# Sharing out half projections between attention steps: three each in the first pair of heads

## Chip, core and metric

The kernel runs on one core of one Trainium2 chip. Its time is device microseconds (us) of one execution; lower is better. The profile comes from one further execution with the hardware profiler on.

## What is computed

One layer of a decoder trunk with 512 tokens of width 1024, in float32. The part that matters here is the first half of it:

```python
h = rms_norm(x, norm_mix[l])
proj = h @ w_in[l]
q_a, k_a, v_a, u_b, gate_b, gate_c, g_a, g_b = jnp.split(proj, split_points, axis=-1)
...
o_a = stick_breaking_attention(heads(q_a), heads(k_a), heads(v_a))   # 8 heads x 64, causal
y_b = gate_b * causal_depthwise_conv(gate_c * u_b, conv_w[l])
branch_a = o_a @ w_branch_a[l]
branch_b = y_b @ w_branch_b[l]
merged = jax.nn.sigmoid(g_a) * branch_a + jax.nn.sigmoid(g_b) * branch_b
x = x + merged @ w_mix_out[l]
```

The attention is

```python
z = jnp.einsum('bhqd,bhkd->bhqk', qb, kb) * scale
mask = k_pos < q_pos
log_fail = jnp.where(mask, jax.nn.log_sigmoid(-z), 0.0)
log_later = lax.cumsum(log_fail, axis=3, reverse=True) - log_fail
weights = jnp.where(mask, jnp.exp(jax.nn.log_sigmoid(z) + log_later), 0.0)
out = jnp.einsum('bhqk,bhkd->bhqd', weights, vb)
```

A softmax cross-attention into 256 memory tokens, a SwiGLU layer and a final RMSNorm follow; the change doesn't touch them.

## The kernel before

**Arithmetic.** Every float32 operand of a matrix product is split into a high and a low part (`..h` and `..l` in tile names; ScalarE casts the high part, VectorE subtracts it for the low part), and each product is three matmuls: high with high, high with low, low with high (`mm3`, lines 154 to 157). Everything is held with channels on the 128 partitions and the 512 tokens along the free axis.

**Projections and halves.** A projection is 128 columns of `w_in`: 8 blocks of 128 input channels, three matmuls each, 24 matmuls into one PSUM tile `pr`. It is cut into two halves of 12 matmuls. `open_project` (line 270) loads the weights (DMA on SP into `wr`, cast to `wh` on ScalarE, `wl` on VectorE) and does the first half; `project` (line 276) does the second, and its caller evicts the PSUM tile on VectorE:

- `qk_part` (line 291): q or k of a pair of heads, scaled and split into `qkh`, `qkl`; for q, the half that belongs to the later 256 tokens is also copied into `lq` by four DMAs on SP (line 300).
- `conv` (line 311), three projections a pair: gate C (`gc`, line 315), the input u (`cu`, lines 321 and 322, then the three taps `cv`, lines 324 to 328), gate B (`gb`, lines 334 and 335, split into `yh`, `yl`).
- `gate` (line 304): merge gate A or B (called A0, B0, A1, B1 below for the first two blocks of 128 channels), evicted into `g` at line 307.

**Attention.** The 8 heads are 4 pairs, and each pair goes through 4 key tiles of 128 keys, from the last to the first: 16 steps (`steps`, line 341). Key tile `kt` has 512 - 128 `kt` queries to serve, so the four steps of a pair grow from 128 to 512 queries. A step has

- `scores` (line 373): TensorE writes z (lines 382 and 389); ScalarE and VectorE make e = log(1 + exp z) from it (lines 396 to 399), GpSimd masks it (`causal`, line 355).
- `parts` (line 408): VectorE adds to e what the key tiles behind it summed up (`carry`, line 420; it comes by a DMA, line 444, issued on SP from a row that `weights` of the step before left), and `lsplit` splits it into `l`: high on ScalarE (line 369), low on VectorE (line 370).
- `weights` (line 428): TensorE adds the cumulative sum of l to z by a triangular matrix (line 433); VectorE takes the next carry from it (line 438), ScalarE exponentiates into `a` (line 441), GpSimd masks, VectorE splits (`ah`, `al`, lines 449 and 450).
- `values` (line 454): TensorE multiplies with v (line 461); after a pair's last step the result `ot` is put together and split (lines 469 to 472).

**Order.** TensorE's order in the attention is the order of the program (`manual_schedule`, line 518). The loop over i, from 0 to 16, does in each iteration: the share of half projections (`fill_some`), `scores` of step i + 1, `weights` of step i, `parts` of step i + 1, `values` of step i - 1. ScalarE, VectorE, GpSimd and SP are ordered by the scheduler of the language when the kernel is built: the chain of a step (`scores`, `parts`, `weights`) has a raised priority, the evictions and splits of the projections have not.

The list `fill` holds 22 projections, so 44 halves, in the order q, k of the next pair, gate C, u, gate B of this pair, pair by pair, and then A0, B0, A1, B1. How many of them are done up to the end of iteration i's share is in two lines:

```python
shares = FILL[0] + (TT - 1) * FILL[1]
...
            fill_some(n_fill * sum(shares[:i + 1]) / sum(shares))
```

`n_fill` is 44; `FILL[0]` is the first pair's four shares, `FILL[1]` that of the other three pairs. `fill_some` goes on while fewer halves are done than its argument, so a fraction is rounded up.

**Buffers.** `pmm` has two PSUM banks. They hold the projections' `pr`, and in iteration 14 (`MEAN_AT`) also two small results on the memory tokens: `rm` (line 526; matmuls at line 188, read on ScalarE at lines 121 and 126), done between the share and the scores, and `rmb` (line 538; matmuls at line 197 into `varb`, read on ScalarE as `ry`, line 121, and on VectorE as `rv`, line 124), done at the iteration's end. `tpool` has seven buffers of 128x512, shared by e, a, qk, gc, cv, gb, g, ot and by the ry, rv and ra of `rmb`. A buffer is given out again when its last reader is done. g of a merge gate stays until its sigmoid, behind the attention.

After iteration 15 there is one more gate projection (line 532), the last values, and then the branches.

Of the kernel before, what the change touches and what calls it, by code (L numbers as in the profile page):

```python
# [29 lines left out]
MEM_AT = (5, 7, 9, 11)  # L30
MEAN_AT = 14
EARLY = 2
FILL = ((3, 2, 3, 3), (2, 2, 3, 4))
WARM = 8
FIRST = 4

# [4 lines left out]
def hybrid_layer(ctx: ExitStack, tc: tile.TileContext, xT_d, memT_d, cols_d, wv_d, win_d,  # L41
# [464 lines left out]
    n_fill = len(fill)  # L506
    shares = FILL[0] + (TT - 1) * FILL[1]

# [585 lines left out]
```

## Time and profile before

| what | value |
|---|---|
| median of three runs | 860.76 us (860.56 to 861.03) |
| the profiled execution | 860.98 us |
| its span, first to last instruction | 859.2 us |
| TensorE matmuls busy | 850.5 us, 99% of the span |
| VectorE busy | 586.5 us, 68% |
| ScalarE busy | 431.1 us, 50% |
| granted TensorE clock, mean | 0.999 |

Times in views of the profile count from the start of the span. The profile records the start of every matmul; the ends are modelled, and consecutive matmuls overlap in it. In a timeline a row has start, length, engine, line, operation, the tile written and those read, the shape, and the count of equal instructions merged into it; in brackets stands how long the engine idled before it and which instruction released it. "PEld" is TensorE's weight load.

### The profile page before, as it was taken

What the parts mean: (1) busy time and instruction counts of PE and PEld (TensorE: products, weight loads), DVE (VectorE), ACT (ScalarE), POOL (GpSimd) and SP (SyncE); (2) the same over time, 40 slices, a digit from 0 to 9 for tenths busy, and PEclk for the clock granted to TensorE, in tenths of its full rate; (3) what the DMA queues carried; (4) which work ended last, traced back from release to release, by engine and by line L of the source; (5) the groups of instructions that cost most, each with busy time, mean ns of one, the idle gap of its engine ahead of it and who ended that gap; (6) DMA issues with size and microseconds to landing.
All of it is one profiled execution on the core that took longest, in us unless ns stands there. A gap on an engine that the chain in (4) does not pass through costs nothing.

```text
span 859.2 us, 12693 instructions
## 1 busy us (share of the span) xinstructions
PE 850.5 (99%) x4912; PEld 748.6 (87%) x4912; DVE 586.5 (68%) x963; ACT 431.1 (50%) x750; POOL 62.0 (7%) x92
## 2 busy tenths in 40 slices
PE   9999999999999999999999999999999999999997
PEld 7877788888888898888888889999999999888897
DVE  8769898986454475555555779888887778533334
ACT  7566766665333344433444666555445556422335
POOL 1011111111000000000000101111111100000002
PEclk9999999999999999999999999999999999999999
DMA  8322331228333255422110527776777753322202
GB/s 295 132 90 77 120 111 62 74 99 266 111 103 111 96 177 184 143 98 98 50 67 33 137 54 202 187 182 172 185 188 195 182 147 127 119 98 99 73 1 98
DMA packets 42859, 108.34 MB, mean 126 GB/s; under 512 B 4656, under 2 KB 8752, under 8 KB 42800
## 3 DMA queue, kind: packets, MB, share of 16 engines
q1 hardware_dynamic: 36528, 95.72, 32.8%
q0 software_dynamic: 5984, 11.54, 8.2%
q8 instruction: 38, 0.62, 0.3%
q10 hardware_dynamic: 288, 0.29, 0.1%
q14 instruction: 21, 0.17, 0.1%
HBM read 104.36 MB, written 2.10 MB: 124 GB/s over the span
## 4 chain that ended last, share of the span: by engine, by line
PE 96%; DVE 2%; DMA 1%; issue 0%; POOL 0%; SPq 0%; DVEq 0%; ACT 0%; POOLq 0%
PE z L801 15%; PE y L801 7%; PE pr L155 7%; PE pr L156 7%; PE pr L157 7%; PE f L156 5%; PE f L157 5%; PE f L155 5%; PE v L801 4%; PE r L156 3%; PE r L155 3%; PE r L157 3%; PE v L261 3%; PE mq L156 2%; PE mq L157 2%; PE mq L155 2%
## 5 line engine op out<-in xcount | busy, mean ns | idle before, releaser
L150 ACT CAST wh<-wr 128x1024 fp32r<-128x1024 f32 x106 | 111.1, 1050 | 222.2 <-issue 98.6
L151 DVE TENSOR_TENSOR wl<-wr,wh 128x1024 fp32r<-128x1024 f32 x106 | 129.4, 1223 | 99.4 <-ACT wh L150 99.2
L155 PE MATMUL pr<-xgh,wh 128*128 128x512 f32 x288 | 112.6, 391 | 0.0
L156 PE MATMUL pr<-xgl,wh 128*128 128x512 f32 x288 | 112.4, 390 | 0.0
L157 PE MATMUL pr<-xgh,wl 128*128 128x512 f32 x288 | 112.3, 390 | 0.0
L156 PE MATMUL f<-actl,wh 128*128 128x512 f32 (+1 forms) x208 | 74.3, 357 | 0.0
L155 PE MATMUL f<-acth,wh 128*128 128x512 f32 (+1 forms) x208 | 74.2, 357 | 0.0
L157 PE MATMUL f<-acth,wl 128*128 128x512 f32 (+1 forms) x208 | 74.1, 357 | 0.0
L801 PE MATMUL z<-xdh,wf 128*128 128x256 f32 x352 | 70.4, 283 | 0.0
L157 PEld LDWEIGHTS pr<-xgh,wl 128*128 128x128 f32 x288 | 54.1, 188 | 11.3
L155 PEld LDWEIGHTS pr<-xgh,wh 128*128 128x128 f32 x288 | 54.1, 188 | 10.9
L156 PEld LDWEIGHTS pr<-xgl,wh 128*128 128x128 f32 x288 | 54.1, 188 | 10.8
L758 POOL DMA_DIRECT2D ws<-in_w_ffn_in_dram x22 | 26.6, 1208 | 469.0 <-DVE c L616 267.8
L801 PEld LDWEIGHTS z<-xdh,wf 128*128 128x128 f32 x352 | 58.0, 192 | 0.0
L821 ACT COPY sa<-z 128x256 f32<-128x256 f32 x44 | 16.4, 372 | 78.3 <-PE z L801 78.2
L801 PE MATMUL z<-xdl,wf 128*128 128x256 f32 x176 | 49.9, 283 | 0.0
L792 DVE TENSOR_TENSOR wf<-s,wf 128x512 fp32r<-128x512 f32 x44 | 30.3, 691 | 21.1 <-ACT wf L791 20.0
L155 PEld LDWEIGHTS f<-acth,wh 128*128 128x128 f32 x208 | 39.3, 189 | 5.8
L156 PEld LDWEIGHTS f<-actl,wh 128*128 128x128 f32 x208 | 39.3, 189 | 5.6
L157 PEld LDWEIGHTS f<-acth,wl 128*128 128x128 f32 x208 | 39.3, 189 | 5.5
L801 PE MATMUL v<-xoh,wf 128*128 128x256 f32 x176 | 35.5, 283 | 0.0
L801 PE MATMUL y<-xch,wf 128*128 128x256 f32 x176 | 35.5, 283 | 0.0
(281 smaller groups left out, 2134.8 us busy)
## 6 DMA issues: line engine op xcount, KB each, us to landing
wr<-in_w_in_dram SPq DMA_DIRECT2D x36, 512.0 KB, 3.3
ws<-in_w_ffn_in_dram SPq DMA_DIRECT2D x22, 512.0 KB, 3.8
wg<-in_w_ffn_in_dram SPq DMA_DIRECT2D x22, 512.0 KB, 4.2
ws<-in_w_ffn_in_dram POOLq DMA_DIRECT2D x22, 512.0 KB, 5.8
wr<-in_w_ffn_out_dram SPq DMA_DIRECT2D x22, 512.0 KB, 3.3
a<-in_w_ffn_in_dram SPq DMA_DIRECT2D x22, 256.0 KB, 4.5
wr<-in_w_branch_dram SPq DMA_DIRECT2D x8, 512.0 KB, 3.2
wr<-in_w_mem_k_dram SPq DMA_DIRECT2D x8, 512.0 KB, 3.2
```

The costliest lines, as they stand in the source:

```text
L150: after(nc.scalar.copy(h2, raw), lead[-1:])
L151: lows.append(nc.vector.tensor_tensor(out=l2, in0=raw, in1=f(h2), op=ALU.subtract))
L155: nc.tensor.matmul(ps, a[0], b[0], start=start, stop=False, **kw)
L156: nc.tensor.matmul(ps, a[0], b[1], start=False, stop=False, **kw)
L157: nc.tensor.matmul(ps, a[1], b[0], start=False, stop=stop, **kw)
L261: nc.tensor.matmul(vps[t], xg[k][a][:, sl], wv[k][b], start=k == 0 and (a, b) == (0, 0), stop=k == KD - 1 and a == 1)
L758: nc.gpsimd.dma_start(s13, a[:, 0:4:3, :], accum_op=ALU.add)
L792: nc.vector.tensor_tensor(out=lo, in0=raw, in1=f(hi), op=ALU.subtract)
L801: nc.tensor.matmul(ps[:, :HS], a, b, start=i < 3 and k == 0 and j == 0, stop=k == KP - 1 and j == 2, skip_group_check=True)
L821: nc.scalar.copy((s[:, :HS], None, None, s[:, HS:], t[:, :HS])[i], z)
```

## The change

```diff
-FILL = ((3, 2, 3, 3), (2, 2, 3, 4))
+FILL = ((3, 3, 3, 3), (2, 2, 3, 4))
```

The shares before add up to 44, the number of halves, so each iteration does just its number. After the change they add up to 45 for the same 44 halves, and with the rounding up the totals behind iterations 0 to 15 are:

```text
before  3 5 8 11   13 15 18 22   24 26 29 33   35 37 40 44
after   3 6 9 12   14 16 19 23   25 27 30 34   36 38 41 44
```

Iteration 1 does three halves instead of two, iteration 15 three instead of four, and all others as many as before. From iteration 1 on every half stands one place earlier. With "o" for the first half of a projection and "f" for the second one, GC, U and GB for the conv's three and q, k numbered by their pair from 0:

```text
i    before                after
0    oq1 fq1 ok1           oq1 fq1 ok1
1    fk1 oGC               fk1 oGC fGC
2    fGC oU fU             oU fU oGB
3    oGB fGB oq2           fGB oq2 fq2
4    fq2 ok2               ok2 fk2
5    fk2 oGC               oGC fGC
6    fGC oU fU             oU fU oGB
7    oGB fGB oq3 fq3       fGB oq3 fq3 ok3
8    ok3 fk3               fk3 oGC
9    oGC fGC               fGC oU
10   oU fU oGB             fU oGB fGB
11   fGB oGC fGC oU        oGC fGC oU fU
12   fU oGB                oGB fGB
13   fGB oA0               oA0 fA0
14   fA0 oB0 fB0           oB0 fB0 oA1
15   oA1 fA1 oB1 fB1       fA1 oB1 fB1
```

No matmul, load or other instruction is added or removed.

## Prediction, made before the changed kernel was run

> **What bounds the kernel now.** I read the page first, for the span, the engines and the chain; then the table by stretch, to see whether the stretch of the change is bound like the rest; then the waits of TensorE there; then the timeline of the attention steps one by one. i is the step loop's counter (line 519); step n is the pair and key tile whose scores are issued in iteration n-1 and whose weights in iteration n.
>
> ```profile
> span 859.2 us, 12693 instructions
> PE 850.5 (99%) x4912; PEld 748.6 (87%) x4912; DVE 586.5 (68%) x963; ACT 431.1 (50%) x750; POOL 62.0 (7%) x92
> PE 96%; DVE 2%; DMA 1%; issue 0%; POOL 0%; SPq 0%; DVEq 0%; ACT 0%; POOLq 0%
> ```
>
> TensorE is busy 99% of the span and carries 96% of the chain. The change adds or removes no matmul, so it can only move the time by what TensorE waits. The stretches, from iteration 0 to the last values (48.26 to 199.55), and behind it:
>
> ```profile
> 48.26:199.55 151.29, 150.32 (x705) 121.90 (x703) 131.43 (x226) 101.45 (x186) 23.69 (x50) 1.00 0.29 97
> 199.55:400.00 200.45, 200.45 (x975) 169.94 (x974) 113.86 (x145) 78.76 (x106) 1.33 (x1) 1.00 0.40 135
> ```
>
> Columns: length, then busy time of TensorE's matmuls, its weight loads, VectorE, ScalarE, GpSimd; granted clock; DMA. Behind 199.55 TensorE never idles for 200 us, so what the attention stretch saves or loses goes to the end unchanged. In the stretch itself TensorE lacks 0.97 us, and VectorE is busy 131.43 of 151.29 us: the chain that each step's weights wait for runs mostly there. Who TensorE waits for in it, by its matmuls and by its weight loads:
>
> ```profile
> PE z L433 <- DVE l L370: 0.9, 2, 0.5
> PEld z L433 <- DVE l L370: 2.1, 4, 0.9
> ```
>
> One line only: the weights' matmuls (line 433) wait for l, the split log terms of their step (line 370, VectorE). Since the ends of matmuls are modelled, 0.9 us is too little; starts are exact, and I measure a wait as the distance between two starts against the same matmuls in a step that doesn't wait. [...]
>
> **What the change removes: two waits.** The share of iteration 1 grows from two halves to three, and every later half moves forward by one place, so that iteration 15 has three instead of four; the other iterations keep their number. The steps that wait now are 0, 1 and 3:
>
> ```profile
> 48.95 0.76 PE L433 MATMUL z<-l,negtri 128*128 128x256 f32 x2
> 49.54 0.39 PE L155 MATMUL pr<-xgh,wh 128*128 128x512 f32 x1
> 55.79 0.49 PE L433 MATMUL z<-l,negtri 128*128 128x512 f32 x1
> 56.72 0.50 PE L433 MATMUL z<-l,negtri 128*128 128x512 f32 x1 [0.43 <-DVE l L370]
> 57.05 0.22 PE L461 MATMUL o<-ah,v 128*128 128x128 f32 x1
> 130.60 0.73 PE L433 MATMUL z<-l,negtri 128*128 128x512 f32 x2
> 131.17 0.22 PE L461 MATMUL o<-ah,v 128*128 128x128 f32 x1
> 55.98 0.68 DVE L370 TENSOR_TENSOR l<-e,l 128x512 fp32r<-128x512 f32 x1
> ```
>
> Step 1: its weights take from 55.79 to 57.05, 1.26 us, where the same two matmuls of step 9 take 0.57 (130.60 to 131.17). So 0.69 us is waiting. Its l is done at 55.98 + 0.68 = 56.66. A half is worth 2.73 us of TensorE (24 matmuls, two halves, from 180.61 to 186.07, rows further down). With one more half ahead of them the weights come at 55.79 + 2.73 = 58.52, 1.86 us behind l: the 0.69 us go. Step 0 (0.59 us from 48.95 to 49.54, against 0.24 for two matmuls of 0.12) keeps its wait of 0.35, since iteration 0 keeps its three halves.
>
> ```profile
> 65.78 0.50 PE L389 MATMUL z<-qkh,qkh 64*128 64x512 f32 x2
> 65.89 0.69 DVE L321 TENSOR_TENSOR cu<-pr,r0b 128x512 f32<-128x512 f32 x1 [1.22 <-PE pr L157]
> 69.79 1.54 DVE L328 SCALAR_TENSOR_TENSOR cv<-cu,gcol,cv 128x512 f32<-128x512 f32 x2
> 76.50 1.02 PE L433 MATMUL z<-l,negtri 128*128 128x512 f32 x3
> 77.25 0.68 DVE L370 TENSOR_TENSOR l<-e,l 128x512 fp32r<-128x512 f32 x1
> 77.99 0.50 PE L433 MATMUL z<-l,negtri 128*128 128x512 f32 x1 [0.47 <-DVE l L370]
> 78.33 0.33 PE L461 MATMUL o<-ah,v 128*128 128x384 f32 x1
> 115.37 1.09 PE L433 MATMUL z<-l,negtri 128*128 128x512 f32 x4
> 116.30 0.33 PE L461 MATMUL o<-ah,v 128*128 128x384 f32 x1
> 139.89 0.50 PE L389 MATMUL z<-qkh,qkh 64*128 64x512 f32 x2
> 149.97 0.69 DVE L370 TENSOR_TENSOR l<-e,l 128x512 fp32r<-128x512 f32 x1
> ```
>
> Step 3: 76.50 to 78.33 is 1.83 us, against 0.93 in step 7 (115.37 to 116.30): 0.90 us of waiting. Iteration 3 keeps three halves, so its cover stays: the scores stand at 65.78, the last of the four weights' matmuls would be due at 76.50 + 0.70 = 77.20, 11.42 us later, and l is done only at 77.93, 12.15 later. What changes is VectorE's work in it. Now the conv input u of pair 0 is finished by the last matmul ahead of the scores, and its chain (cu 65.89 to cv 71.33) stands in front of the step's own. In the changed order u is finished one half earlier, and the open half of gate B comes between. Pair 2 has that order already (iteration 10 is open u, finish u, open gate B; iteration 11 starts with finishing gate B), and there l is done at 149.97 + 0.69 = 150.66, 10.77 us behind the scores of 139.89. That is 0.65 us ahead of the 11.42. So I take 0.90 us off; the bounds are 0 (the old 12.15 stays) and 0.90. How VectorE and ScalarE order their instructions is decided anew when the kernel is built, so none of these distances is safe to a few tenths.
>
> **What it moves: iterations 4 to 14.** Same numbers of halves, other neighbours. Of the moved projections every weight load goes along in the same order, on SP, ScalarE (cast) and VectorE (subtract); the copies of q's second half (line 300, SP) of pairs 2 and 3 fall one half earlier, so they stand less in the way of the carry DMA of line 444 than now. I cost that at nothing: the cover is the two or more halves between a step's scores and its weights. The thinnest cover now is step 13's:
>
> ```profile
> 167.89 0.68 DVE L370 TENSOR_TENSOR l<-e,l 128x512 fp32r<-128x512 f32 x1
> 168.57 0.73 PE L433 MATMUL z<-l,negtri 128*128 128x512 f32 x2
> ```
>
> l is done at 168.57, and the second of the two matmuls, which needs it, starts 0.33 later. One VectorE instruction of 0.69 us (such as the gate's eviction, below) placed ahead costs 0.36 us; one fewer costs nothing. I take 0 and keep 0.36 for the range.
>
> **What it adds: the last step with three halves, and a bank.**
>
> ```profile
> 177.77 0.17 PE L188 MATMUL var<-mean_r,acch 128*128 128x2 f32 x1
> 178.20 0.50 PE L389 MATMUL z<-qkh,qkh 64*128 64x512 f32 x2
> 178.54 0.69 DVE L307 TENSOR_TENSOR g<-pr,r0b 128x512 f32<-128x512 f32 x1
> 180.49 0.28 PE L197 MATMUL varb<-accl,mean_r 128*128 128x256 f32 x1
> 180.61 0.40 PE L155 MATMUL pr<-xgh,wh 128*128 128x512 f32 x1
> 182.66 0.55 DVE L450 TENSOR_TENSOR al<-a,ah 128x384 fp32r<-128x384 f32 x1
> 183.49 0.41 DVE L124 TENSOR_SCALAR rv<-varb 128x256 f32<-128x256 f32 x1
> 185.68 0.56 DVE L450 TENSOR_TENSOR al<-a,ah 128x384 fp32r<-128x384 f32 x1
> 186.07 0.39 PE L155 MATMUL pr<-xgh,wh 128*128 128x512 f32 x1
> 187.09 0.69 DVE L370 TENSOR_TENSOR l<-e,l 128x512 fp32r<-128x512 f32 x1
> 191.52 1.10 PE L433 MATMUL z<-l,negtri 128*128 128x512 f32 x4
> ```
>
> Cover of step 15: scores at 178.20, weights at 191.52, 13.32 us; without one half 10.59. l is done at 187.78, 9.58 behind the scores. 1.01 us are left, so this costs nothing (bounds: 0, and 0.86 if l took the 12.15 us of step 3, against the 11.29 at which the last matmul is due).
>
> The bank: the memory means of iteration 14 (lines 526 and 538) take their PSUM tile from the same two banks as the projections. Now no projection is half open there. In the changed order the first half of gate A1 is, and holds one bank from ahead of L188 until A1 is evicted. So the two means and gate B1 share the other. First, L188 needs gate B0 evicted: the projection ends 2.73 us before it, and the eviction now comes 0.77 behind its end and is done 1.46 behind (177.77 to 179.23), so it is in time; I take 0, the bound is 1.46 (eviction done as late as now). Second, B1's first matmul needs varb read. TensorE gets there one half behind 180.61, at 183.34; the last read, rv, ends at 183.90. That is a new wait of 0.56 us, 0.6 with the signal. Queued behind it on TensorE are all of B1, step 15's weights and the rest. Its bounds: 0 (rv a little earlier), and 3.31: rv needs one of the seven buffers of tpool, now gets it from the first al of step 14 (182.66), and would end at 186.24 + 0.41 = 186.65 if it got it from the second (185.68).
>
> **The sum.** -0.69 - 0.90 + 0.60 = -0.99 us. The profiled execution took 860.98 us for its span of 859.2, 0.22 above the median 860.76 of three runs; it becomes 859.99, and the median 859.8. That is 0.11%, less than the 0.2% (1.72 us) that a measurement of this kernel can tell from no change. With the bounds of its own terms (no bank wait: 859.2; bank wait and step 13: 860.1; step 3 keeping half its wait: 860.6) the forecast's own range is 859.2 to 860.6.
>
> **The rivals.** One: both waits go, the bank is read in time, and in the new order step 0 loses its 0.35 too: -1.94 us, 858.8. For it: rv misses by only 0.56 us. Against: nothing of the change touches iteration 0. Two: the last step's cover is too short after all: -1.59 + 0.60 + 0.86 + 0.36 = +0.23, 861.0; the 9.58 us speak against it. Three, slower: the bank that the half-open A1 holds becomes the bound of iterations 14 and 15. VectorE has the eviction of B0 behind the l of its step, as now (1.46 us), and rv behind the second al (3.31 us): -1.59 + 4.77 = +3.18, 863.9. It decides as soon as these two waits exceed 1.59 us, and shows as slower from 3.31 on. For it: VectorE is 87% busy and takes the gates and rv as low-priority work between the chain's instructions, and A0, B0, two e, two a and the mean's ry fill the seven buffers just then. Against: now the same seven are full and rv still gets the first. [...]
>
> **How the numbers follow.** Forecast 0.45, rival one 0.18, rival two 0.10, rival three 0.27 in a size that shows. Forecast and rival two lie within 0.2%: 0.55. The likeliest is 859.8 us. The range goes down to rival one, 858.8, and up into rival three to 863.0, leaving its worst part, less than 2 in 10, outside.
>
> **What would show it.** The weights of step 1 should take 0.57 us and those of step 3 0.93 from first start to the values; step 0 keeps its 0.59. TensorE's wait list should lose line 370 but for step 0, and gain a wait of a pr matmul (line 155, gate B1) on VectorE's rv or ScalarE's ry of varb, some 0.6 us, between two gate projections just ahead of the last weights. Step 15's l should end some 9.6 us behind its scores, with no wait at its weights. The stretch behind the last values should be as long as now. I am wrong if step 3 still waits (the conv chain wasn't the reason), if L188 starts late behind B0's projection, if any of steps 5, 9, 10, 13 waits for line 370, or if time changes behind the attention.

## Result, and the profile after

The changed kernel takes 863.68 us (median of 8 runs, 862.33 to 865.77) against 860.92 us before (8 runs, 860.56 to 861.13). The ratio is 1.0033, 95% interval 1.0021 to 1.0045: slower by 2.8 us, where 1.0 us less was forecast, and outside the range that was given. The runs don't lie around one value: four are at 862.3 to 862.5 with a mean granted clock of 0.998 or 0.999, and four at 864.9 to 865.8 with 0.995 to 0.997. The profiled execution (862.49 us, span 860.8) is one of the first four.

Both waits that were to go did go. From the timeline of TensorE in the changed kernel, the weights of steps 1 and 3 and what follows them:

```profile
58.38 0.73 PE L433 MATMUL z<-l,negtri 128*128 128x512 f32 x2
58.95 0.22 PE L461 MATMUL o<-ah,v 128*128 128x128 f32 x1
...
78.39 1.09 PE L433 MATMUL z<-l,negtri 128*128 128x512 f32 x4
79.33 0.33 PE L461 MATMUL o<-ah,v 128*128 128x384 f32 x1
```

Step 1's weights take 0.57 us and step 3's 0.94, as in the steps that never waited. But the wait list of TensorE over the whole span has one new line, a projection that waits for VectorE's rv (the other line is the start of the kernel):

```profile
PE pr L155 <- DVE rv L124: 2.9, 1, 2.9
PE warm L220 <- DVE neg L87: 1.6, 1, 1.6
```

It stands in iteration 15 between gate A1 and gate B1. TensorE's timeline there, and VectorE's over the same stretch:

```profile
179.19 0.49 PE L389 MATMUL z<-qkh,qkh 64*128 64x512 f32 x2
...
181.60 0.40 PE L155 MATMUL pr<-xgh,wh 128*128 128x512 f32 x1
...
184.12 0.39 PE L157 MATMUL pr<-xgh,wl 128*128 128x512 f32 x1
187.45 0.50 PE L155 MATMUL pr<-xgh,wh 128*128 128x512 f32 x1 [2.95 <-DVE rv L124]
...
193.04 1.10 PE L433 MATMUL z<-l,negtri 128*128 128x512 f32 x4
```

```profile
183.16 0.56 DVE L450 TENSOR_TENSOR al<-a,ah 128x384 fp32r<-128x384 f32 x1
183.63 0.68 DVE L399 SCALAR_TENSOR_TENSOR e<-z,e 128x512 f32<-128x512 f32 x1
184.23 0.35 DVE L449 CAST ah<-a 128x384 fp32r<-128x384 f32 x1
184.61 0.56 DVE L420 TENSOR_TENSOR e<-e,carry 32x384 f32<-32x384 f32 x1
185.20 0.69 DVE L399 SCALAR_TENSOR_TENSOR e<-z,e 128x512 f32<-128x512 f32 x1
185.81 0.55 DVE L450 TENSOR_TENSOR al<-a,ah 128x384 fp32r<-128x384 f32 x1
186.39 0.55 DVE L420 TENSOR_TENSOR e<-e,carry 32x384 f32<-32x384 f32 x1
186.97 0.42 DVE L124 TENSOR_SCALAR rv<-varb 128x256 f32<-128x256 f32 x1
...
188.38 0.69 DVE L370 TENSOR_TENSOR l<-e,l 128x512 fp32r<-128x512 f32 x1
```

The last matmul of A1 starts at 184.12 and the first of B1 at 187.45, where 184.35 was due (matmuls follow each other by 0.23 us here): 3.10 us late. The matmuls right behind the wait are a little slower as well: from 181.60 to 193.04 the iteration's three halves take 11.44 us, where three halves of 2.73 take 8.19, so the loss is 3.25 us. B1 needs the PSUM bank of varb, and rv, its last reader, ends at 187.39. In the kernel before, rv (183.49) came ahead of the second of the two e and both carry additions:

```profile
183.82 0.67 DVE L399 SCALAR_TENSOR_TENSOR e<-z,e 128x512 f32<-128x512 f32 x1
184.53 1.12 DVE L420 TENSOR_TENSOR e<-e,carry 32x384 f32<-32x384 f32 x2
```

In the changed kernel it comes behind them and the second al. The step's three halves were cover enough: l ended 9.9 us behind its scores (179.19 to 189.07), and the weights at 193.04 didn't wait.

So the profiled execution is explained: -0.69 - 0.90 + 3.25 = +1.66 us, less 0.16 by which its first steps came earlier, and the span grew by 1.5 (859.24 to 860.78). The upper four runs lie another 2.4 to 3.3 us higher; the experiments deal with them.

### The profile page after: what moved, and what is told of

Its sections match the earlier page's. It is cut to its first block, busy times and chain, and to the rows that moved or that the text cites. A ratio compares the mean times of both kernels' runs of the same rounds, so it can differ in the third digit from the quotient of the medians.

```text
span 860.8 us, 12694 instructions
## 1 busy us (share of the span) xinstructions
PE 850.4 (99%) x4912; PEld 748.6 (87%) x4912; DVE 586.5 (68%) x963; ACT 430.7 (50%) x750; POOL 64.6 (7%) x92
## 4 chain that ended last, share of the span: by engine, by line
PE 98%; DVE 1%; ACT 0%; issue 0%; POOL 0%; DVEq 0%; POOLq 0%
PE z L801 15%; PE pr L155 7%; PE pr L157 7%; PE pr L156 7%; PE y L801 7%; PE f L156 5%; PE f L157 5%; PE f L155 5%; PE v L801 4%; PE r L156 3%; PE r L157 3%; PE r L155 3%; PE v L261 3%; PE mq L157 2%; PE mq L155 2%; PE br L157 2%
```

## Experiments

Theory A: the bank. A1 held half open over the two memory means leaves one bank for both means and B1, and the price is set by where rv stands in VectorE's order. Theory B: the upper runs have a stretch of half clock on TensorE, which the long wait brings. Rivals: the last step's cover is too short; rv waits for one of the seven shared buffers; the upper runs have another cause.

**The tail alone.** Kernel before, one half moved from iteration 15 into iteration 14:

```diff
-    shares = FILL[0] + (TT - 1) * FILL[1]
+    shares = (3, 2, 3, 3, 2, 2, 3, 4, 2, 2, 3, 4, 2, 2, 4, 3)
```

> The kernel before with one half moved from iteration 15 into iteration 14 (A1 half open across the two memory means) and nothing else moved. Bank theory: the first matmul of gate B1 waits for varb's last read on VectorE, 3.0 to 3.4 us as in the changed kernel; the waits of steps 1 (0.69) and 3 (0.90) stay; span 859.2 + 3.3 = 862.5, faster group of the runs near 864.2. Cover rival (the last step's three halves are too short for its l): the wait stands at the weights of step 15, line 433, not at a projection, and is below 1 us; span below 860.2. Clock theory: a part of the runs lies another 2 to 3 us higher at a lower mean clock (0.995 to 0.997), as in the changed kernel; if that part came from the moved projections of the other iterations instead, no run here shows it.

865.50 us (5 runs, 864.23 to 866.08) against 861.31 (23 runs), ratio 1.0046 [1.0034, 1.0058]. The wait list of TensorE has both:

```profile
PE pr L155 <- DVE rv L124: 2.9, 1, 2.9
PE warm L220 <- DVE neg L87: 1.6, 1, 1.6
PE z L433 <- DVE l L370: 0.9, 2, 0.5
```

The same 2.9 us as in the changed kernel, and the two old waits, at the same places: what the change loses is all in this one half of A1. The cover rival falls: step 15's weights don't wait. Two runs lie at 864.2 to 864.4 with a clock of 0.999, three at 865.5 to 866.1 with 0.997.

**The half taken elsewhere.** Three halves in iteration 1, and iteration 11 has three instead of four, so that the last pair stands as before:

```diff
-    shares = FILL[0] + (TT - 1) * FILL[1]
+    shares = (3, 3, 3, 3, 2, 2, 3, 4, 2, 2, 3, 3, 2, 2, 3, 4)
```

> Three halves in iteration 1, and the half is taken from iteration 11 (three instead of four), so that iterations 12 to 15 stand as before and no projection is half open at the memory means. Bank theory: steps 1 and 3 lose their 1.59 us of waiting, step 11 has 0.6 us of margin left, B1 doesn't wait: span 857.6, median 859.3, and no second group of runs. Cover rival: one half less before a pair's last step costs 0.5 to 0.9 us at the weights of step 11: 859.9 to 860.2. If the gain of steps 1 and 3 were given back later anyway: 860.9.

861.52 us (11 runs) against 861.31, ratio 1.0004 [0.9995, 1.0012]: nothing gained. Steps 1, 3 and 11 don't wait, and neither does B1, but step 13, which the prediction had named as the thinnest, does. TensorE's waits and VectorE's timeline in iteration 13:

```profile
PE z L433 <- DVE l L370: 0.7, 1, 0.7
PE z L433 <- ACT l L369: 0.4, 1, 0.4
```

```profile
164.35 0.67 DVE L470 TENSOR_TENSOR ot<-o,ot 64x512 f32<-64x512 f32 x1
164.96 0.67 DVE L399 SCALAR_TENSOR_TENSOR e<-z,e 128x512 f32<-128x512 f32 x1
165.66 0.69 DVE L470 TENSOR_TENSOR ot<-o,ot 64x512 f32<-64x512 f32 x1
166.38 0.42 DVE L420 TENSOR_TENSOR e<-e,carry 32x256 f32<-32x256 f32 x1
166.84 0.69 DVE L334 TENSOR_TENSOR gb<-pr,r0b 128x512 f32<-128x512 f32 x1
167.44 0.68 DVE L170 TENSOR_TENSOR ol<-ot,oh 128x512 fp32r<-128x512 f32 x1
168.04 0.69 DVE L370 TENSOR_TENSOR l<-e,l 128x512 fp32r<-128x512 f32 x1
```

The end of pair 2 (ot, ol) and a gate B eviction have come in between the step's own instructions; l ends at 168.73. From start to start, step 13 loses 1.46 us, nearly all of the 1.59 gained. The iterations 12 to 15 do the same halves as before, so only the order differs. My expectation had given this outcome a time (860.9, the gain given back later), but had not named step 13.

**The means one iteration earlier.** Changed kernel with

```diff
-MEAN_AT = 14
+MEAN_AT = 13
```

> The changed kernel with the two memory means in iteration 13 instead of 14, where no projection is half open; iteration 15 keeps its three halves. Bank theory: no wait at B1; 1.59 us gained: span 857.6, median 859.3, one group of runs. Cover rival: a wait at the weights of step 15 remains, 0.5 us or more: 859.8 and above. Clock theory: no run at a lower mean clock, since no idle stretch of 3 us is left.

864.75 us (6 runs, 862.23 to 865.71) against 861.31, ratio 1.0036 [1.0023, 1.0048]. Expected was a gain. TensorE waits again at a projection, now gate B0, and for ScalarE; ScalarE's timeline shows why:

```profile
PE pr L155 <- ACT rv L126: 2.7, 1, 2.7
```

```profile
170.55 0.86 ACT L396 ACTIVATE e<-z 128x384 f32<-128x384 f32 x2
171.30 0.94 ACT L397 ACTIVATE e<-e 128x384 f32<-128x384 f32 x2
172.46 0.60 ACT L441 ACTIVATE a<-z 128x512 f32<-128x512 f32 x1 [0.23 <-DVE carry L438]
172.95 0.93 ACT L398 ACTIVATE e<-e 128x384 f32<-128x384 f32 x2
173.78 0.25 ACT L121 ACTIVATE ry<-var,eps_t 128x2 f32<-128x2 f32 x1
173.92 0.26 ACT L126 ACTIVATE rv<-var,eps_t 128x2 f32<-128x2 f32 x1
```

The first mean, of a few columns, was written by 169.5, and ScalarE reads it at 173.78, behind two score chains. One bank is held by it, the other by varb, and B0 gets none. So theory A has to be put more widely: a half-open projection isn't needed. Two banks serve both means and the projections, and whichever result is read late stops TensorE.

**rv first.** Changed kernel, with everything that ScalarE and VectorE do for `rmb` (ry, rv, ra) at a raised priority:

```diff
-                rmb = mean[1]("rmb", bank=mmtile)
+                with tc.high_priority(300):
+                    rmb = mean[1]("rmb", bank=mmtile)
```

> The changed kernel with a raised priority for the reading of varb, so that rv stands on VectorE ahead of the scores' two max-and-add instructions of step 15 instead of behind them; bank and halves as in the changed kernel. Order theory (the bank costs 3.3 us only because rv comes late in VectorE's order): the wait at B1 falls from 3.1 to 0.2 to 0.6 us, span 857.8 to 858.3, median 859.5 to 860.0. If the wait comes from the seven buffers that rv waits for, it stays above 1.5 us. Clock theory: one group of runs; the second group goes with the long wait.

860.06 us (11 runs, 859.26 to 860.51) against 861.31, ratio 0.9985 [0.9977, 0.9994]. VectorE and TensorE at that place:

```profile
184.27 0.35 DVE L449 CAST ah<-a 128x384 fp32r<-128x384 f32 x1
184.54 0.42 DVE L124 TENSOR_SCALAR rv<-varb 128x256 f32<-128x256 f32 x1
184.87 0.68 DVE L399 SCALAR_TENSOR_TENSOR e<-z,e 128x512 f32<-128x512 f32 x1
```

```profile
184.76 0.39 PE L157 MATMUL pr<-xgh,wl 128*128 128x512 f32 x1
185.01 0.50 PE L155 MATMUL pr<-xgh,wh 128*128 128x512 f32 x1
```

rv stands ahead of both e, ends at 184.96, and B1 starts at 185.01 without a gap (0.25 us from start to start; the weight load shows 0.3 us of waiting). Bank, halves and cover are those of the changed kernel. The place of rv in VectorE's order was worth the whole loss but 0.2 us (the three halves take 8.37 us), and with it the change is the gain that the prediction described. It is the fastest of the kernels run, faster than both the kernel before (by 1.25 us) and the changed one.

**rv in memory of its own.** Changed kernel, `keep=accm[:, 1, :]` added to the call of `rmb`:

> The changed kernel with rv written to memory of its own (half of the finished accm tile) instead of one of the seven shared buffers. Buffer rival (rv comes late because it waits for a buffer): the wait at B1 falls from 3.1 us to about 0.6, time near 860.0. Order theory (rv comes late because VectorE's order places it behind the chain's instructions): the wait stays at 2.9 to 3.2 us, and the time lies near 862.4, or near 865 with a half clock.

865.72 us (one run), and the wait is as before, now for a tile that needs no shared buffer:

```profile
PE pr L155 <- DVE accm L124: 2.9, 1, 2.9
```

rv stands at the same place in VectorE's order. The buffer rival falls: the prediction's bound of 3.31 us had nearly the right size for the wrong reason.

**A longer wait.** Changed kernel, rv computed three times over:

```diff
-                nc.vector.tensor_scalar(out=v, in0=var, scalar1=EPS, scalar2=None, op0=ALU.add)
+                for _ in range(3 if s == "rmb" else 1):
+                    nc.vector.tensor_scalar(out=v, in0=var, scalar1=EPS, scalar2=None, op0=ALU.add)
```

> The changed kernel with rv computed three times over (same values), so that varb's bank is held some 2.1 us longer (two more of 0.42 us and the chain's two l subtractions of 0.69 between them). Clock theory: the idle stretch of TensorE grows from 3.1 to about 5.2 us, and now every run has at least one 3.41 us stretch at half clock behind it, which costs 1.6 us more each: 862.4 + 2.1 + 1.6 = 866.1 or above, no run near 864.5. If the slower group were unrelated to the wait, runs would still split, with about half of them near 864.5.

866.50 us (4 runs, 865.79 to 867.59) against 861.47, ratio 1.0059 [1.0045, 1.0073]; TensorE waits 4.9 us, and all four runs have a clock of 0.995 to 0.997.

```profile
PE pr L156 <- DVE rv L125: 4.9, 1, 4.9
```

No run near 864.5, as theory B has it; the lowest is 0.3 below what I gave.

**The changed kernel again.**

> The changed kernel, unaltered, on this call's chip. Clock theory: its runs fall into two groups some 2.5 us apart, and those of the upper group show a mean clock of 0.995 to 0.997 against 0.998 to 0.999; a profile of the upper group has a stretch at clock 0.5 right behind the wait at B1. If the groups come from the chip of the first measurement, only one appears here.

865.31 us (4 runs, 864.38 to 865.63) against 861.47. All four belong to the upper group (clock 0.995 to 0.997), so these runs alone show no two groups; but the profile is now one of that group. The table by stretch, where the third column from the right is the granted clock, and the numbers ahead of it are the length and the busy times of TensorE's matmuls, its weight loads, VectorE, ScalarE and GpSimd:

```profile
186.00:187.00 1.00, 0.00 (x0) 0.00 (x0) 0.97 (x3) 1.00 (x2) 0.12 (x1) 1.00 0.00 0
187.00:188.50 1.50, 0.13 (x1) 0.13 (x2) 1.41 (x4) 0.69 (x2) 0.43 (x1) 1.00 0.00 0
188.50:191.90 3.40, 3.40 (x9) 2.62 (x10) 3.40 (x7) 0.07 (x1) 0.00 (x0) 0.50 0.02 5
191.90:195.00 3.10, 3.10 (x15) 2.58 (x14) 0.48 (x1) 0.00 (x0) 0.00 (x0) 0.99 0.45 160
```

TensorE is empty from 185.4 to 188.4, starts B1, and its granted clock is 0.50 for 3.4 us (188.50 to 191.90). The three halves around the wait take 13.01 us (182.52 to 195.53) against 11.44 in the first profile: 1.6 us for one such stretch. In the profile of the kernel with rv in its own memory the clock is 0.51 from 187.00 to 188.50, 0.50 to 191.90 and 0.69 to 195.00, some 6.8 us of half clock by these shares, and the three halves take 14.30 us (181.91 to 196.21): 2.9 us for the longer stretch.

The span of this profile is 2.5 us longer than the first one's (863.3 against 860.8), and only 1.6 of it is the half clock behind the wait. The rest is lost at the start. The same group of matmuls starts 0.94 us apart, first profile above, this one below:

```profile
7.27 1.07 PE L261 MATMUL v<-wvh,xgl 128*128 128x512 f32 x4
```

```profile
8.21 1.08 PE L261 MATMUL v<-wvh,xgl 128*128 128x512 f32 x4
```

**Work in the wait.** Changed kernel, twelve matmuls of constants between A1 and B1, into a score bank whose content is no longer needed:

```diff
+    def gate_busy(m, j):
+        gate(m, j)
+        ps = ztile("busy")
+        for _ in range(12):
+            nc.tensor.matmul(ps, neg1, neg1[:, None, :].broadcast_to([P, S // P, P]), start=True,
+                             stop=True)
...
-            fill_up((O_A, O_B)[j] + m * P, gate, m, j)
+            fill_up((O_A, O_B)[j] + m * P, gate_busy if (m, j) == (1, 0) else gate, m, j)
```

> The changed kernel with twelve matmuls of constants into a free score bank between gate A1 and gate B1, where TensorE would only wait for varb (their results are read by nobody). They take 2.7 us inside the wait, so B1 starts no later. Clock theory (half clock comes from TensorE being idle for about 3 us): the wait that is left is below 0.6 us, no run has a mean clock below 0.998, and all lie in the faster group, 862.3 to 863.3. If the second group came from the lateness itself or from the memory system, runs near 865 remain. If the matmuls don't fit in the wait, the time is some 0.5 us higher.

863.06 us (11 runs, 862.35 to 863.37) against 861.33. B1 is as late as ever, but TensorE idles 0.2 us, all eleven runs have a clock of 0.998 or more, and the upper group is gone:

```profile
PE pr L155 <- DVE rv L124: 0.2, 1, 0.2
```

So with B1 as late as before but TensorE busy, 0 of 11 runs have a clock below 0.998, against 8 of the 12 runs of the changed kernel: the lower clock goes with the idleness, not with the lateness.

**A wait in between.** Changed kernel, the raise of priority 100 instead of 300:

> The changed kernel with a lower raise of the priority for varb's reading: rv stands on VectorE ahead of the second carry addition and the second al, and behind both max-and-add instructions. Order theory: the wait at B1 is 1.8 to 2.2 us, between the 3.1 us of the changed kernel and the 0.3 us of the kernel with the higher raise; 861.2 to 862.0. Clock theory: an idle stretch of 2 us is too short, all runs at a mean clock of 0.998 or more; if any wait of this order could bring the half clock, some runs lie 1.5 us higher.

863.65 us (11 runs, 861.26 to 864.05) against 861.33, ratio 1.0020 [1.0011, 1.0028].

```profile
PE pr L155 <- DVE rv L124: 1.8, 1, 1.8
```

The wait is the expected one, but it wasn't too short: 7 of the 11 runs have a clock of 0.997 and lie at 863.6 to 864.1, the other four at 861.3 to 862.2.

**Four halves first.** Kernel with rv first, and

```diff
-    shares = FILL[0] + (TT - 1) * FILL[1]
+    shares = (4, 3, 3, 3, 2, 2, 3, 3, 2, 2, 3, 4, 2, 2, 3, 3)
```

> As the kernel with the raised priority for varb's reading, with four halves in iteration 0 and three in iteration 7: shares 4 3 3 3, 2 2 3 3, 2 2 3 4, 2 2 3 3. If step 0's wait of 0.35 us goes, and step 7 (cover 10.7 us, l so far 9.9 behind its scores) doesn't wait: span 858.0, 0.35 us below that kernel, some 1.6 us (0.19%) below the kernel before. Rival: another order of VectorE in iterations 1 to 6 gives a new wait of 0.3 to 1 us, and nothing is gained over that kernel.

861.31 us (11 runs) against 861.47, ratio 0.9998 [0.9989, 1.0007]. Step 0's wait is gone, but steps 3 and 7 wait together 1.6 us longer than their matmuls need (1.1 and 0.5 us). That is the rival, but larger than the 0.3 to 1 us that I gave it, and in part at step 7, which had lost a half: against the kernel with rv first, nothing is gained.

## Why the prediction was wrong

- The removed waits, -0.69 and -0.90: right, both to 0.01 us. So, as far as the order shows, was the reason given for step 3: u's chain came earlier and l ended 9.73 us behind the scores, ahead of the 11.42. No experiment took that order apart from the rest.
- Iterations 4 to 14 at nothing, L188 at nothing, the last step's cover at nothing: right in the changed kernel. So was the time behind the attention: from step 15's weights to the end it is 667.7 us in both. In the kernel where the third pair gives the half, step 13 did wait, 1.46 us, so that margin was thin, and the 0.36 us kept for it too little.
- The bank: the place, the instruction waited for and the mechanism were right; the size failed. The step reads "TensorE gets there one half behind 180.61, at 183.34; the last read, rv, ends at 183.90", and takes 0.60 us. That end was read in the old order of VectorE, although the same text says that the order is decided anew at the build. Measured: 3.25 us. The upper bound, 3.31, was in the text, but worked out from a buffer, which the kernel with rv in its own memory ruled out; that it came out so near is in part luck. The cause is rv's place in the order, as raising its priority showed. Why the scheduler moved rv behind the carry additions isn't known; it wasn't tried.
- The half clock: at nothing in the sum. Behind the wait of 2.9 us the clock was 0.50 for 3.4 us in the second profile of the changed kernel, which cost 1.6 us; with a wait of 1.8 us (rv midway) 7 of 11 runs had a mean clock of 0.997. Four of the first eight runs have 0.995 to 0.997, and there it adds, as an estimate from the two profiles, 1.6 us, or 2.9 with the longer stretch. So it makes the median: the four runs without it lie at 862.3 to 862.5, still inside the range.

The sum thus failed at the bank's term, 0.60 us for what took 3.25, which turned the gain into a loss, and the half clock, at nothing, took the time out of the range. Rival three, with 0.27, is what happened in the main: slower, from the bank, with rv behind the second al. Of its 4.77 us the first part, 1.46 for the eviction of gate B0, didn't come, since L188 started without a wait; the second, 3.31, came as 3.25, and the clock on top.

## What to carry to other kernels

When work that holds a scarce PSUM bank is moved, price the wait by the latest place that the reader can get in its engine's order, not by the place that it has now; and look for whatever low-priority read releases the bank, because raising that one read can be the whole fix. A wait of TensorE was not just its length here: with a wait of 1.8 us 7 of 11 runs had a lower mean clock as well, with 2.9 us 12 of 18, so one profile without it proves little. And a margin of a few tenths in a step that nobody touched isn't a margin, as long as the order of other engines is free.

## What the runs showed of the hardware

In five of the twelve profiles the granted clock is below 1.00 in or right behind TensorE's wait at a projection (second table). How often, by the idle time that the profile names, counting runs with a mean clock below 0.998 (none of 59 runs of the kernel before lies there; the rows come from several chips; rv midway and work in the wait from the same one):

| idle of TensorE in one place | runs with a mean clock below 0.998 |
|---|---|
| 0 to 0.2 us (rv first; work in the wait) | 0 of 22 |
| two waits of up to 0.7 us, at steps 3 and 7 (four halves first) | 0 of 11 |
| 0.4 and 0.7 us within 1.6 us (third pair gives) | 2 of 11 |
| 1.8 us (rv midway) | 7 of 11 |
| 2.7 us (means in iteration 13) | 5 of 6 |
| 2.9 us (changed, twice; tail alone; rv own) | 12 of 18 |
| 4.9 us (rv three times) | 4 of 4 |

From the row of the third pair to that of 2.9 us some runs have the lower clock and some don't. For the rows of the third pair and of rv midway the profiled run has a mean clock of 0.998, so there the count rests on the mean clock of the other runs alone (0.997).

The profiles of the kernels with a wait of 1.8 us or more, with the granted clock in the stretches in or behind the wait:

| kernel | wait of TensorE | granted clock |
|---|---|---|
| rv midway | 1.8 us | mean of the run 0.998 |
| changed, first profile | 2.9 us | 1.00 from 182.00 to 196.00 |
| means in iteration 13 | 2.7 us | 0.82 from 171.70 to 174.20, 0.50 to 180.10, 1.00 to 183.00 |
| rv own | 2.9 us | 1.00 from 186.00 to 187.00, 0.51 to 188.50, 0.50 to 191.90, 0.69 to 195.00 |
| tail alone | 2.9 us | 0.88 from 182.00 to 196.00 |
| changed, again | 2.9 us | 1.00 from 187.00 to 188.50, 0.50 to 191.90, 0.99 to 195.00 |
| rv three times | 4.9 us | 1.00 from 184.40 to 189.20, 0.50 from 189.30 to 192.60, 1.00 from 192.70 to 195.00 |

The changed kernel has both, with the same wait of 2.9 us: 1.00 throughout in its first profile, 0.50 behind the wait in the second. That fits its two groups of runs. What decides between the two isn't shown: no run varied the place of a wait alone.
